# Longer unbroken runs of the dense products, and other TensorE times in the planner, in a hybrid attention and delta-rule layer

## The chip, the cores and the metric

One core of a Trainium2 chip runs the kernel. The metric is the device time of one execution in microseconds. The engines of the core are TensorE (PE, matmuls; PEld is its weight load), VectorE (DVE), ScalarE (ACT), GpSimd (POOL) and SyncE (SP, which issues DMAs). Each engine works through its own list of instructions in order, and waits at an instruction whose operands are not there.

## What is computed

A decoder layer on 512 tokens and 16 meta tokens, width 1024. Two branches of eight heads each run on the same normalised input: differential softmax attention, and a gated delta rule in chunks. Their gated outputs are merged and projected.

```python
proj = hn @ w_in
aq, ak, av, az, dq, dk, dv, dz, db, da, ga, gd = split(proj)
# attention branch, per head: two softmaxes, their difference times v
pd = p[:, :, 0] - lam * p[:, :, 1]
y_a = (rms_norm(pd @ v) * (1 - lam_init) * silu(az)) @ w_branch_attn
# delta branch: causal convolution of width 4, silu, normalised q and k, then in chunks
m = where(strict, (kb @ k.T) * decay, 0)
t_inv = triangular_solve(m + eye, eye)
u = t_inv @ (v * beta);  w = t_inv @ (kb * exp(gc))
# over the chunks, one after the other
v_new = u - w @ state
o = q_dec @ state + a_intra @ v_new
state = state * chunk_decay + k_dec.T @ v_new
y_d = (rms_norm(o) * silu(dz)) @ w_branch_delta
merged = sigmoid(ga) * y_a + sigmoid(gd) * y_d
out = rms_norm(h + merged @ w_out)
```

## The kernel before

**Products.** Each dense product takes one block of 128 columns of the weights (name and number in `ORDER`, such as dz(2): the delta branch's gate of head 2). Input and weights are split in a high and a low part (`hnH`, `hnL`; `wh` made by ScalarE, `wl` by VectorE, line 383), and three passes of 8 matmuls each make one accumulator: 24 matmuls for a segment of tokens. Gates and queries take one segment of 512 columns; keys and values two, of 272 and 256. `dense()` (line 1580) makes the products one after the other: for each pair of heads g dk, dv, dq of both heads, then ak, aq, az, av of head 2g, then dz(2g) and dz(2g+1), then ak, aq, az, av of head 2g+1. After the four pairs come gd and yd (the delta branch's output product), ga and ya, and the output projection. The generator yields the engine ahead of every three matmuls; between two yields another task may put its own instructions in.

**The delta rule of a pair** (`delta_pair`, line 853). `MT` holds the products of keys with keys times the decay `E`, evacuated by VectorE; it goes to DRAM (`scrm`) and comes back in another layout (`msub`). VectorE then inverts triangular blocks of 32 x 32 by substitution: 31 steps of two operations (`tmps`, `ts`), each needing the one before. The result goes by DRAM (`scrt`) to `td`. The first matmuls on it are `td,MT`; blocks of 64 and 128 (`TT`), the chunks (`vin`, `u`, state `S`) and the output follow: ScalarE copies to `MT`, squares, VectorE reduces and scales, TensorE transposes (`ident,MT`), VectorE makes `od`. `qT<-qT,eg` multiplies the queries by the decay `eg`, which a DMA broadcasts from DRAM (`gcd`) once `eg`'s one buffer is free.

**The two ends.** `branch` (line 1508) splits `od` in `brH` (ScalarE) and `brL` (VectorE) for yd. The buffers for it lie in a pool that opens when all four pairs are done (`pools`, line 1691), so all eight splits follow the last `od`.

**What sets the order.** `Plan` (line 75) is a list scheduler, run while the kernel is built: at each point the task goes on that can start soonest by an estimate of the instructions' times (`Engine.time`, line 220), and of several that of the lowest rank. Delta tasks have rank 0, attention 2, the dense products 4, so they fill what the others leave. The order that results is fixed in each engine's list. The estimates have no part in the run itself. In the profile, helper line 216 stands for every instruction issued through `Engine`.

Of the kernel before, what the change touches and what calls it, by code (L numbers as in the profile page):

```python
# [20 lines left out]
KB = D // P  # L21
# [15 lines left out]
def dense_order():  # L37
    """Products with weight blocks of 128 columns, in the order in which they are made."""
    order = []
    for g in range(H // 2):  # L40
        for n in ("dk", "dv", "dq"):
            order += [(n, 2 * g), (n, 2 * g + 1)]
        order += [(n, 2 * g) for n in ("ak", "aq", "az", "av")]
        order += [("dz", 2 * g), ("dz", 2 * g + 1)]
        order += [(n, 2 * g + 1) for n in ("ak", "aq", "az", "av")]
    for g, y in (("gd", "yd"), ("ga", "ya")):
        order += [(g, c) for c in range(AHEAD)]
        for c in range(KB):
            order += [(y, c)] + [(g, c + AHEAD)] * (c + AHEAD < KB)
    return order  # L50
# [4 lines left out]

# how many of the accumulators serve a purpose at most, and how many there are
BANKS = dict(pd=2, pat=2, pdl=2)
# [4 lines left out]

# tiles of each kind, and accumulators, that are in use at a time
SLOTS = dict(raw=3, w=2, wo=4, psc=1, xp=2, y=2, kT=2, qT=2, ktd=2, vr=2, E=2, eg=1, AT=2, MT=2, sc=2, km=1,
             ts=1, msub=1, TT=1, aq=2, ak=1, vT=1, vs=1, e=4, pT=2, pm=2, ao=1, br=8, th=4)


# until when the tensor engine's clock runs at half its rate
COLD = 10500
# [8 lines left out]
class Plan:  # L78
    """Puts the instructions of many tasks in one order, which all engines keep.

    A task is a generator. It yields the engine that its next instructions are for and then emits them; or an event's
    name, to wait for that; or (name,), to wait for one of some slots. The task that can start soonest goes on, by an
    estimate of the instructions' times in ns; of several, the one of the lowest rank.
    """

# [11 lines left out]
    def here(self):  # L97
        """When and where that is done which the running task has emitted."""
        if self.arrival:
            return self.arrival, SP  # L100
        return (self.end, self.engine) if self.engine else (self.task.time, self.task.src)
# [44 lines left out]
    def settle(self):  # L146
        """Lets every task go on that waits for what is there."""
        moved = True
        while moved:
            moved = False  # L150
            for task in sorted(self.tasks, key=lambda t: t.rank):
                if task.want == ():
                    self.wait(task, (0.0, SP))
                elif isinstance(task.want, tuple):
                    kind = task.want[0]
                    free = self.slots["bank" if kind in self.kinds else kind]
                    if not free or self.kinds.get(kind) == 0:
                        continue
                    if kind in self.kinds:
                        self.kinds[kind] -= 1  # L160
                    free.sort()
                    *since, task.slot = free.pop(0)
                    self.wait(task, tuple(since))
                elif task.want in self.events:
                    self.wait(task, self.events[task.want])
                else:
                    continue
                moved = True
# [22 lines left out]
class Banks(list):  # L191
    """The accumulators of a product, in the order in which they are done."""

# [7 lines left out]
class Engine:  # L201
    """An engine whose instructions' times are estimated as they are emitted."""

# [16 lines left out]
    def time(self, op, args, kw):  # L220
# [4 lines left out]
        n = int(np.prod(out.shape[1:]))  # L225
        if self.name == PE:
# [3 lines left out]
            if dt == F32:  # L230
                small = ins[0].shape[0] <= 64
                return 2 * max(2 * n / 2.4, 27 if small else 107)
            if dt == F32R:
                return n / 2.4 + 2.7 if n >= 256 else max(2 * n / 2.4, 107)
            return n / 2.4 + 57
# [15 lines left out]
def hybrid_block(ctx: ExitStack, tc: tile.TileContext, x, meta, wblk, wbd, wout, pcol, prow, out):  # L251
# [30 lines left out]
    def bank(kind):  # L282
        """An accumulator, two banks for scores, else one: that which the running task has taken."""
        return mk(ps, [P, 2, 512], F32, kind, SLOTS[kind]) if kind == "psc" else banks_[plan.task.slot]
# [16 lines left out]

    # ---------------------------------------------------------------- constants
    nwb = mk(sp, [P, D], F32, "nwb")
# [75 lines left out]

    # ---------------------------------------------------------------- loads  # L380
    weights = {}

    def split(n, raw):
        """Weights as high and low parts."""
        if n < len(ORDER) or n - len(ORDER) in (4, 5):
# [52 lines left out]

    # ---------------------------------------------------------------- hn, transposed, as high and low parts
    hn = [hnp.tile([P, KB, L], F32R, tag=t, name=t) for t in ("hnH", "hnL")]  # L440

    def normalise(n):
        """The meta tokens lie as (part of the channels, token) on the partitions, the others by token."""
        yield f"x{n}"
# [53 lines left out]

    # ---------------------------------------------------------------- gates of the delta rule, all heads
    FULL = [(0, 272), (272, 256)]  # L500
# [11 lines left out]
    def gates():  # L512
# [137 lines left out]
        spawn(rows())  # L650
        # the meta tokens of two heads lie on 32 partitions
        msel = gt("msel", (32, 8, 2))
# [47 lines left out]

    # ---------------------------------------------------------------- what follows a projection
    od = [rp.tile([P, SEQ], F32, tag=f"od{h}", name=f"od{h}") for h in range(H)]
# [10 lines left out]
    def conv_silu(banks, chan, t_lo, dst_tag, tags=("pd", "pd")):  # L713
        """2 silu(conv(projection)) from t_lo on, in a tile of dst_tag or in that returned second, else scratch"""
        n = L - t_lo
# [45 lines left out]
    def after_gate(h, banks, dst, event):  # L761
        """dst = 2 silu(projection)"""
        pd = banks[0][0]
# [85 lines left out]

    # ---------------------------------------------------------------- the delta rule, two heads at a time  # L850
    kt_, s_, sd_, vs_, qe_ = 0, 1, 2, 3, 4

    def delta_pair(gi):
# [14 lines left out]
        def decay(i):  # L868
            """exp(gc_j - gc_i), keys on partitions"""
            h = hs[i]  # L870
# [16 lines left out]
        def keys(i):  # L887
# [23 lines left out]
            def decayed():  # L911
                """The keys' part in the state at the end of their chunk"""
                for c in range(NC):
# [184 lines left out]

        # inverses of the unit triangular 32 x 32 blocks, a block and half its columns on a partition
        yield ("ts",)  # L1100
# [39 lines left out]
        tdt, tdmt = mk(dp, [P, 8, 32], F32, "tdt", 1), mk(dp, [32, 32], F32, "tdmt", 1)  # L1140
        # blocks of 32 to 64 to 128, transposed; x is head and chunk
        TT = slot(dp, [P, 8, P], F32, "TT")
# [213 lines left out]

    # ---------------------------------------------------------------- differential attention, one head
    def attention(h):
# [11 lines left out]
        def combine(i, st, es):  # L1370
# [7 lines left out]
            give("e")  # L1378
            # the meta tokens' part, of which a high part, a high part and a low part lie beside one another
            yield ("pm",)  # L1380
# [118 lines left out]

    # ---------------------------------------------------------------- the dense products  # L1500
    def again(tag, dt=F32):
# [6 lines left out]
    def branch(h, of, name):  # L1508
        """A branch's result as high and low parts."""
        yield f"{'od' if name == 'yd' else 'oa'}{h}"  # L1510
# [42 lines left out]
    def first_products():  # L1553
        """The first two products, in parts that follow the tokens' arrival."""
        yield ("psc",)
# [24 lines left out]
    def dense():  # L1580
        yield from first_products()
        for n, (name, i) in list(enumerate(ORDER))[2:]:
# [6 lines left out]
            for t0, nn in SEGS.get(name, BODY):  # L1589
                yield ("pd",)  # L1590
                pd = None
                for k in range(KB):
                    yield PE
                    pd = bank("pd")[:, :nn] if k == 0 else pd
# [16 lines left out]
            if name in ("yd", "ya"):  # L1611
                tick(name, KB)
                if i == KB - 1:
                    for _ in range(H):
                        give("br")
        # the output projection, the residual and the last norm
        yield "gp"
# [24 lines left out]
    def finish(hf, tb, c0, c1, pd, tag, ssq, fnw, xr):  # L1642
        """The residual's sum and its square's; with the last columns of some tokens, their norm"""
        t = xr[hf, tb][:, c0:c1]
# [15 lines left out]
        spawn(weigh(), 2)  # L1660
        # of the sums so far, but the last: mean + eps
        if col == 0:
# [28 lines left out]
    def pools():  # L1691
        """The pools that take the place of those of the two branches."""
        yield "delta"
# [41 lines left out]
def layout(inputs):  # L1735
    """The inputs as the program reads them: moved, and nothing else."""
    f = {k: np.asarray(v) for k, v in inputs.items()}
# [41 lines left out]
```

## Time and profile before

| | |
|---|---|
| three runs | 787.58, 789.86, 791.32 us (median 789.86) |
| the profiled execution's span | 787.3 us |
| TensorE's first product matmul, last matmul's end | 7.8 us, 781.1 us |
| VectorE, ScalarE, GpSimd busy | 541.8, 383.3, 76.1 us |
| substitutions (first `tmps` to last `ts`), us from the start | 90.0 to 128.4, 227.4 to 262.4, 355.4 to 392.5, 489.3 to 525.5 |
| first `td,MT` of each pair | 136.9, 272.0, 401.1, 533.2 us |

The profiled execution has a span and no time of its own beside it; the runs' times are of other executions. A window row gives a stretch in us from the start and, per engine, how long it was busy in it. A wait row has the total, the number and the longest. A timeline row has start, duration, engine, line, operation, output<-inputs, shapes and count, and in brackets the idle time ahead of it with what ended it. Matmuls overlap, so that a matmul's duration (0.39 us) is longer than the distance to the next one.

### The profile page before, as it was taken

Reading aid. Unit: us, or ns where it says so; the run is one execution under the profiler, and the core shown is the slowest. Engines: PE = TensorE matmul, PEld = TensorE weight load, DVE = VectorE, ACT = ScalarE, POOL = GpSimd, SP = SyncE. Lnnn points to the kernel's source line nnn. Section 1 sums busy time; section 2 is a strip of 40 time slices with the busy share of each in tenths; the row PEclk is TensorE's granted clock in tenths of the full one; section 3 lists DMA queues with packets and bytes.
Section 4 is the critical chain, followed back from the end, with each engine's and each line's share of the span. In section 5 each row is a group of like instructions: output and inputs, shape, how many; then the busy total and the mean of one; then the engine's idle time right before and its main releaser. Section 6 shows DMA issues by size and latency. Waiting matters only on the chain.

```text
span 787.3 us, 13576 instructions
## 1 busy us (share of the span) xinstructions
PE 761.1 (97%) x5191; PEld 682.8 (87%) x5191; DVE 541.8 (69%) x1279; ACT 383.3 (49%) x944; POOL 76.1 (10%) x114
## 2 busy tenths in 40 slices
PE   5999999999999999999999999899999999999996
PEld 4999878999988899987999998788888888888886
DVE  6788697788779778859968875995772334335643
ACT  5374535576545557553557744355562224223322
POOL 3120002021100301100030201000000000000001
PEclk9999999999999999999999999999999999999999
DMA  7132624202352401272240125233116232233402
GB/s 274 40 110 84 152 81 110 68 28 82 95 141 81 122 28 55 67 153 83 81 110 28 56 90 119 81 94 83 51 62 235 80 108 88 100 100 112 136 1 107
DMA packets 46744, 74.36 MB, mean 94 GB/s; under 512 B 20528, under 2 KB 29136, under 8 KB 46680
## 3 DMA queue, kind: packets, MB, share of 16 engines
q1 hardware_dynamic: 45400, 69.18, 29.3%
q0 software_dynamic: 1280, 4.33, 2.5%
q8 instruction: 40, 0.66, 0.3%
q14 instruction: 24, 0.20, 0.1%
HBM read 65.98 MB, written 3.19 MB: 88 GB/s over the span
## 4 chain that ended last, share of the span: by engine, by line
PE 57%; DMA 5%; DVE 4%; issue 1%; ACT 1%; SPq 1%; POOL 1%; POOLq 0%; DVEq 0%; ACTq 0%
PE bank L216 55%; DMA msub<-scrm 2%; PE psc L216 2%; DVE wl L216 1%; DMA scrt<-ts 1%; DMA td<-scrt 1%; SPq L216 1%; DVE tmps L216 1%; DVE ts L216 1%; DMA eg<-gcd 1%; DMA scrm<-MT 1%; DVE aq L216 0%; POOL ts L216 0%; DVE MT L216 0%; ACT wh L216 0%
## 5 line engine op out<-in xcount | busy, mean ns | idle before, releaser
L216 PE MATMUL bank<-hnH,wh 128*128 128x512 f32 (+3 forms) x944 | 317.6, 339 | 1.4 <-ACT hnH L216 0.8
L216 PE MATMUL bank<-hnH,wl 128*128 128x512 f32 (+3 forms) x944 | 302.9, 323 | 3.7 <-DVE wl L216 3.7
L216 PE MATMUL bank<-hnL,wh 128*128 128x512 f32 (+3 forms) x944 | 302.4, 323 | 0.0
L216 PEld LDWEIGHTS bank<-hnH,wl 128*128 128x128 f32 x944 | 177.7, 189 | 19.6 <-DVE wl L216 5.5
L216 PEld LDWEIGHTS bank<-hnH,wh 128*128 128x128 f32 x944 | 177.8, 189 | 15.0 <-ACT hnH L216 1.0
L216 PEld LDWEIGHTS bank<-hnL,wh 128*128 128x128 f32 x944 | 178.0, 190 | 11.1
L216 ACT CAST wh<-raw 128x1024 fp32r<-128x1024 f32 x98 | 102.8, 1049 | 127.0 <-PE bank L216 116.2
L216 DVE TENSOR_TENSOR wl<-raw,wh 128x1024 fp32r<-128x1024 f32 x98 | 120.0, 1225 | 61.4 <-ACT wh L216 60.8
L216 DVE SCALAR_TENSOR_TENSOR y<-xp,pc,y 128x528 f32<-128x528 f32 (+1 forms) x72 | 54.3, 755 | 0.8 <-ACT y L216 0.2
L216 PE MATMUL bank<-brH,wh 128*128 128x512 f32 x128 | 50.1, 392 | 0.0
L216 PE MATMUL bank<-brL,wh 128*128 128x512 f32 x128 | 49.8, 389 | 0.0
L216 PE MATMUL bank<-brH,wl 128*128 128x512 f32 x128 | 49.8, 389 | 0.0
L216 ACT ACTIVATE e<-psc,ast 128x144 f32<-128x144 f32 (+3 forms) x64 | 34.4, 541 | 30.3 <-DVE ast L216 26.2
L216 DVE TENSOR_TENSOR tmps<-msub,ts 97x240 f32<-97x240 f32 (+27 forms) x124 | 39.5, 319 | 5.9 <-DMA msub<-scrm 4.1
L216 DVE TENSOR_TENSOR ts<-ts,tmps 97x240 f32<-97x240 f32 (+27 forms) x124 | 39.6, 320 | 1.8
L216 PE MATMUL psc<-ak,aq 128*128 128x264 f32 (+3 forms) x160 | 29.1, 304 | 4.3 <-ACT e L216 4.3
L216 POOL DMA_DIRECT2D ak<-ak x16 | 8.8, 551 | 219.5 <-DVE ak L216 161.2
L216 PEld LDWEIGHTS psc<-ak,aq 128*128 128x128 f32 x160 | 23.6, 189 | 7.2 <-ACT e L216 6.0
L216 DVE SCALAR_TENSOR_TENSOR od<-th,bank 128x512 f32<-128x512 f32 x16 | 10.9, 684 | 26.6 <-PE bank L216 26.6
L216 DVE TENSOR_REDUCE ast<-psc 128x1 f32<-128x528 f32 (+3 forms) x40 | 28.5, 713 | 0.2
L216 PEld LDWEIGHTS bank<-brH,wh 128*128 128x128 f32 x128 | 24.0, 188 | 5.1
L216 PEld LDWEIGHTS bank<-brH,wl 128*128 128x128 f32 x128 | 24.0, 188 | 5.1
(299 smaller groups left out, 1214.6 us busy)
## 6 DMA issues: line engine op xcount, KB each, us to landing
raw<-in_wblk_dram SPq DMA_DIRECT2D x96, 512.0 KB, 3.5
ak<-ak POOLq DMA_DIRECT2D x16, 264.0 KB, 4.3
raw<-in_wout_dram SPq DMA_DIRECT2D x8, 512.0 KB, 3.7
xt<-in_x_dram SPq DMA_DIRECT2D x4, 512.0 KB, 3.6
E<-gcd SPq DMA_DIRECT2D x8, 256.0 KB, 5.7
eg<-gcd SPq DMA_DIRECT2D x8, 256.0 KB
xr<-in_x_dram SPq DMA_DIRECT2D x8, 256.0 KB, 6.5
out_dram<-xr SPq DMA_DIRECT2D x8, 256.0 KB, 2.1
```

The source lines that it names most:

```text
L216: return real(*args, **kw)
```

## The change

All comments and docstrings are taken out, which moves lines (216 becomes 219) and nothing else. A constant `RUN = 4` is new. `dense()` yields to the planner less often: ahead of each segment of under 512 tokens once (24 matmuls in one run), and in a product of 512 tokens ahead of every fourth k (two runs of 12). The planner's estimates for TensorE's matmuls are other numbers: 512 columns 231.8 ns (216 before), 272 columns 125 (116), 256 columns 117.9 (109.4), and three nanoseconds more on each of the two passes of a float32 matmul. Slots, ranks, the other engines' estimates and what is computed stay.

```diff
+RUN = 4
...
             if dt == F32:
                 small = ins[0].shape[0] <= 64
-                return 2 * max(2 * n / 2.4, 27 if small else 107)
+                return 2 * max(2 * n / 2.4 + 3, 27 if small else 110)
             if dt == F32R:
-                return n / 2.4 + 2.7 if n >= 256 else max(2 * n / 2.4, 107)
+                return 0.445 * n + 4 if n >= 240 else 111
...
                 for k in range(KB):
-                    yield PE
+                    if k % (KB if nn < 512 else RUN) == 0:
+                        yield PE
                     pd = bank("pd")[:, :nn] if k == 0 else pd
```

Since the planner makes the order, the change shows in the engines' lists. Three places of them follow. A row is an instruction: the line, the operation, output<-inputs with the number of the tile, and the shape.

**TensorE at the first `td,MT`, pair 0.** Before: it stands behind all of av(1) (`wh_1534` is av(1)'s weight block, here the end of its second segment).

```order
L216 MATMUL bank_6_83<-hnH,wl_1536 128x256
L216 MATMUL bank_5_82<-ident,pm_87_618 96x128
L216 MATMUL bank_6_83<-hnH,wh_1534 128x256
L216 MATMUL bank_6_83<-hnL,wh_1534 128x256
L216 MATMUL bank_6_83<-hnH,wl_1536 128x256
L216 MATMUL bank_1_78<-td_1604,MT_953 32x32 x4
L216 MATMUL bank_1_78<-td_1604,MT_997 32x32 x4
```

After: the block ahead of it is az(1)'s (512 columns), followed by scores of head 1's attention.

```order
L219 MATMUL bank_6_83<-hnH,wh_1458 128x512
L219 MATMUL bank_6_83<-hnL,wh_1458 128x512
L219 MATMUL bank_6_83<-hnH,wl_1460 128x512
L219 MATMUL psc_1607<-ak_1020,aq_1075 128x264 x4
L219 MATMUL bank_4_81<-td_1555,MT_946 32x32 x4
L219 MATMUL bank_4_81<-td_1555,MT_996 32x32 x4
```

The 48 matmuls of av(1) have moved from ahead of `td,MT` to behind it. In the other pairs `td,MT` stood inside the next pair's dk(4) (pair 1) or inside av's second segment (pairs 2 and 3); now it stands ahead of av(2g+1) in all of them.

**VectorE at the last evacuations of `MT`, pair 0.** `MT_997` before and `MT_996` after are that of head 1; `qT_918` and `qT_901` are the queries of head 0; `E_1014` and `E_1003` the decay of the next pair. Before:

```order
L216 SCALAR_TENSOR_TENSOR MT_997<-bank_3_80,sc_635,E_651 128x128
L216 TENSOR_TENSOR ak_1029<-vT_939,ak_1029 64x528
L216 SCALAR_TENSOR_TENSOR MT_997<-bank_3_80,sc_635,E_651 128x128
L216 SCALAR_TENSOR_TENSOR MT_997<-bank_5_82,sc_635,E_651 128x128
L216 TENSOR_TENSOR AT_998<-bank_3_80,E_651 128x256
L216 SCALAR_TENSOR_TENSOR MT_997<-bank_5_82,sc_635,E_651 128x128
L216 TENSOR_TENSOR ak_1029<-vT_939,ak_1029 64x528
L216 TENSOR_TENSOR qT_918<-qT_918,eg_1018 128x512
L216 TENSOR_SCALAR E_1014<-E_1014,gc 128x128
```

After, from the second evacuation on:

```order
L219 SCALAR_TENSOR_TENSOR MT_996<-bank_3_80,sc_638,E_654 128x128
L219 TENSOR_TENSOR ak_1020<-vT_934,ak_1020 64x528
L219 TENSOR_TENSOR AT_997<-bank_3_80,E_654 128x256
L219 TENSOR_SCALAR sc_638<-sc_638 128x4
L219 TENSOR_TENSOR qT_901<-qT_901,eg_1004 128x512
L219 TENSOR_SCALAR E_1003<-E_1003,gc 128x128
L219 TENSOR_TENSOR ak_1020<-vT_934,ak_1020 64x528
L219 TENSOR_SCALAR E_1003<-E_1003,gc 128x128
L219 SCALAR_TENSOR_TENSOR MT_996<-bank_5_82,sc_638,E_654 128x128
L219 TENSOR_SCALAR E_1003<-E_1003,gc 128x128
L219 SCALAR_TENSOR_TENSOR MT_996<-bank_5_82,sc_638,E_654 128x128
```

The product with `eg` and three rows of the next decay have moved ahead of the last two evacuations.

**TensorE at the end of the delta rule.** Before, from the last transposes `ident,MT` to product yd(0) (`brH`); `wh_6739` is gd(2), `wh_6869` gd(3), of which the rows of one step are shown.

```order
L216 MATMUL bank_2_79<-ident,MT_5857 128x128 x4
L216 MATMUL bank_4_81<-ident,pm_86_617 96x128
L216 MATMUL bank_1_78<-hnH,wh_6739 128x512
L216 MATMUL bank_1_78<-hnL,wh_6739 128x512
L216 MATMUL bank_1_78<-hnH,wl_6741 128x512
L216 MATMUL bank_4_81<-vm_619,pmT_6924 128x128
L216 MATMUL bank_4_81<-vs_6629,pT_6923 128x128 x3
L216 MATMUL bank_3_80<-hnH,wh_6869 128x512
L216 MATMUL bank_3_80<-hnL,wh_6869 128x512
L216 MATMUL bank_3_80<-hnH,wl_6871 128x512
```

After, from the state's product of the last chunk to yd(0); `wh_6842` is the weight block of yd(0):

```order
L219 MATMUL bank_4_81<-S_6880,qT_5790 128x128
L219 MATMUL bank_4_81<-u_6958,AT_5826 128x128
L219 MATMUL bank_1_78<-ident,e_6815 128x128 x3
L219 MATMUL bank_6_83<-ident,pm_86_627 96x128
L219 MATMUL bank_6_83<-vm_628,pmT_6935 128x128
L219 MATMUL bank_6_83<-vs_6653,pT_6934 128x128 x3
L219 MATMUL bank_3_80<-ident,MT_5825 128x128 x4
L219 MATMUL bank_2_79<-ident,e_6893 128x128 x4
L219 MATMUL bank_4_81<-ident,pm_85_626 96x128
L219 MATMUL bank_4_81<-vm_628,pmT_7000 128x128
L219 MATMUL bank_4_81<-vs_6653,pT_6999 128x128 x4
L219 MATMUL bank_5_82<-brH_7014,wh_6842 128x512
```

The 24 matmuls of gd(3) have moved from behind the last `ident,MT` to ahead of the last chunk's `vin,TT`.

## The prediction

> **What bounds the kernel now.** I read the engine shares on the page first, then its chain, then TensorE's waits, then windows. Times of steps are us from the start of the profiled execution.
>
> ```profile
> span 787.3 us, 13576 instructions
> PE 761.1 (97%) x5191; PEld 682.8 (87%) x5191; DVE 541.8 (69%) x1279; ACT 383.3 (49%) x944; POOL 76.1 (10%) x114
> PE 57%; DMA 5%; DVE 4%; issue 1%; ACT 1%; SPq 1%; POOL 1%; POOLq 0%; DVEq 0%; ACTq 0%
> ```
>
> TensorE is busy 97% of the span. The matmuls are the same after the change, so its work stays; what can move is the time in which it waits. The chain leaves TensorE for some 10% of the span, through DMA and VectorE. TensorE's largest waits behind its start, and two ways to count them by stage (20 us windows; below them windows from the first matmul of product dz(2g), g the head pair, to the first td,MT):
>
> ```profile
> PE psc L216 <- ACT e L216: 4.3, 3, 1.9
> PE bank L216 <- DVE wl L216: 3.7, 4, 1.5
> PE bank L216 <- DMA td<-scrt: 1.4, 3, 0.7
> ```
>
> ```profile
> 100.00:120.00 20.00, 18.10 (x101) 15.67 (x100) 18.60 (x54) 7.59 (x23) 0.00 (x0) 0.91 0.27 84
> 500.00:520.00 20.00, 18.67 (x113) 16.32 (x112) 19.69 (x61) 7.97 (x25) 0.00 (x0) 1.00 0.29 97
> 600.00:620.00 20.00, 20.00 (x89) 16.34 (x88) 5.59 (x5) 4.23 (x6) 0.00 (x0) 1.00 0.36 113
> 92.10:136.90 44.80, 42.55 (x248) 36.74 (x246) 39.01 (x107) 20.36 (x51) 5.11 (x8) 0.96 0.34 93
> 225.60:272.00 46.40, 44.42 (x277) 38.91 (x275) 40.55 (x113) 23.91 (x57) 5.41 (x8) 1.00 0.36 99
> 357.20:401.10 43.90, 42.08 (x243) 36.20 (x241) 39.94 (x110) 21.62 (x52) 4.65 (x7) 0.96 0.32 93
> 490.80:533.20 42.40, 38.83 (x229) 33.26 (x228) 38.30 (x107) 19.04 (x47) 1.02 (x2) 1.00 0.33 92
> ```
>
> The columns are the window, its length, then busy us of PE, PEld, DVE, ACT, POOL, and the granted clock. In 500:520 VectorE is busy 19.69 of 20 us: this is the substitution (62 rows tmps and ts, each using the one before), with the weight splits wl, softmax and scores between its rows. There, four times in the kernel, VectorE sets the pace. In 600:620 it is busy 5.59 and TensorE all 20.00.
>
> **Longer runs.** The deleted comments emit nothing. A step of three matmuls becomes one of 12 or 24. What a switch between products costs TensorE is in the spacing of starts:
>
> ```profile
> 93.66 0.39 PE L216 MATMUL bank<-hnH,wh 128*128 128x512 f32 x1
> 93.90 0.39 PE L216 MATMUL bank<-hnL,wh 128*128 128x512 f32 x1
> 130.14 0.29 PE L216 MATMUL bank<-hnL,wh 128*128 128x272 f32 x1
> 132.91 0.29 PE L216 MATMUL bank<-hnH,wl 128*128 128x272 f32 x1
> ```
>
> 512 columns take 0.231 us here (0.24 in this pair, 20.00/89 = 0.225 in 600:620), 272 columns (132.91 − 130.14)/22 = 0.126, and 256 columns 0.118, all inside runs already. Over the listing a matmul behind a switch is late by at most 0.01 us, and 200 switches vanish at most: 0 to −2, taken −0.5. The planner's new figures, 0.232 and 0.125, fit these rows; the old, 0.216 and 0.116, were 7% short.
>
> The Trainium skill, page "TensorE: Matmul & The Clock Gate", section "Back-to-back issue gap", gives columns/2.4 + 2.5 ns, 0.216 us at 512: the planner's old number. The rows above (0.225 to 0.24) do not agree, and by that rule alone the new costs would be the worse ones; the sum here doesn't use it.
>
> **The substitution's result comes sooner in TensorE's queue.** td,MT takes the substitution's result by DRAM. By the listings, between dz(2g)'s first matmul and td,MT there stood, in pair 0, 96 of 512 columns (dz, dz, aq, az), ak's 24 + 24, av's 24 + 24 and 48 small ones: 96 x 0.231 + 2 x 24 x (0.126 + 0.118) + 48 x 0.13 = 40.1. In pairs 1 to 3: 43.5 (with 18 of dk besides), 39.3 and 37.8 (9 of av's second part). After, av stands behind td,MT in every pair, with 31 to 35 small ones before it: **32.4, 32.4, 32.4, 31.9**. The windows took 44.8, 46.4, 43.9, 42.4, so 4.7, 2.9, 4.6, 4.6, in all **16.8 us**, are waits, small gaps and a lower clock (0.91 in 100:120: half speed for 3.4 us, 1.7 lost; the same once in pair 2). Work ahead of the substitution is the same in both.
>
> So TensorE will be at td,MT 5.4 to 11 us sooner. Is its input there? Before:
>
> ```profile
> 81.04 0.69 DVE L216 TENSOR_TENSOR qT<-qT,eg 128x512 f32<-128x512 f32 x1 [3.55 <-ACT eg L216]
> 76.42 0.34 DVE L216 SCALAR_TENSOR_TENSOR MT<-bank,sc,E 128x128 f32<-128x128 f32 x1
> 82.26 0.29 DVE L216 TENSOR_SCALAR E<-E,gc 128x128 f32<-128x128 f32 x1 [0.53 <-DMA E<-gcd]
> 90.00 0.19 DVE L216 TENSOR_TENSOR tmps<-msub,ts 97x31 f32<-97x31 f32 x1 [0.32 <-DMA msub<-scrm]
> 128.20 0.17 DVE L216 TENSOR_TENSOR ts<-ts,tmps 97x16 f32<-97x16 f32 x1
> 227.36 0.18 DVE L216 TENSOR_TENSOR tmps<-msub,ts 97x31 f32<-97x31 f32 x1
> 262.27 0.17 DVE L216 TENSOR_TENSOR ts<-ts,tmps 97x16 f32<-97x16 f32 x1
> 355.44 0.19 DVE L216 TENSOR_TENSOR tmps<-msub,ts 97x31 f32<-97x31 f32 x1 [2.56 <-DMA msub<-scrm]
> 392.34 0.18 DVE L216 TENSOR_TENSOR ts<-ts,tmps 97x16 f32<-97x16 f32 x1
> 489.26 0.19 DVE L216 TENSOR_TENSOR tmps<-msub,ts 97x31 f32<-97x31 f32 x1 [1.25 <-DMA msub<-scrm]
> 525.32 0.17 DVE L216 TENSOR_TENSOR ts<-ts,tmps 97x16 f32<-97x16 f32 x1
> 136.91 0.87 PE L216 MATMUL bank<-td,MT 32*32 32x32 f32 x25 [0.36 <-DMA td<-scrt]
> 533.16 0.81 PE L216 MATMUL bank<-td,MT 32*32 32x32 f32 x23 [0.69 <-DMA td<-scrt]
> ```
>
> The input came just when TensorE did: the waits there are 0.36 and 0.69. Its path has three lengths.
>
> Start: last MT evacuation, scrm to DRAM, msub back, then tmps. Pair 0: 76.76 to 90.00, 13.2 us; the others 13.1, 13.8, 12.4. After, in pair 0, qT stands ahead of the second head's last two MT, and qT waits for the transfer eg (3.55 here), with E's transfer behind it. qT's end at 81.73, two E, ak (0.7), MT at 0.3 each put the last MT at 83.3 instead of 76.8, the substitution at 83.3 + 13.2 = 96.5; if eg came sooner by 5.0, which is its mean wait, 91.5. Nothing decides between them: I take the middle, 94.0. In pair 2 qT moves ahead too, with two E: 0.69 + 2 x 0.28 = +1.2, 356.6. In pairs 1 and 3 it stood there before; fewer rows ahead of MT give −1.8 (225.6) and −0.2 (489.1).
>
> Length: 38.4, 35.1, 37.1, 36.2. The listing has 106 other rows in the four substitutions instead of 142; 36 rows at some 0.45 us are 16 us. By pair 31.0, 32.0, 32.1, 32.5.
>
> End to td,MT: through scrt, 136.91 − 128.37 = 8.5; 9.6, 8.6 and 7.7 in the others.
>
> Input against TensorE's arrival:
> pair 0: 94.0 + 31.0 + 8.5 = 133.5, arrival 92.1 + 32.4 = 124.5, wait 9.0.
> pair 1: 225.6 + 32.0 + 9.6 = 267.2 against 258.0, wait 9.2.
> pair 2: 356.6 + 32.1 + 8.6 = 397.3 against 389.6, wait 7.7.
> pair 3: 489.1 + 32.5 + 7.7 = 529.3 against 522.7, wait 6.6.
> In all 32.5. The old 16.8 lie ahead of td,MT and are swallowed; so is a later weight split wl (in pair 1 that of dz(2) now stands behind the first rows tmps), as long as TensorE waits less than 9 us for it. So the difference is **+15.7**. TensorE's in-order queue holds av(2g+1), dk and dv of the next pair behind td,MT: none can fill the wait. The bounds: each substitution 3 us sooner, +3.7; 2 us later, +23.7.
>
> The skill's same page, section "Part 1: The HAM clock gate", has the clock halved after an idle window of about 3.4 us; 0.91 in 100:120 agrees. After waits of 7 to 9 us it would add up to 1.7 us each, 7 in all, inside the range.
>
> **The end of the delta rule.** Before, gd3's 24 matmuls (5.5 us) stood behind the last transposes ident,MT and covered the split of od into brH and brL, which yd0 reads; after, gd3 is done ahead of the last chunk's vin,TT.
>
> ```profile
> 565.06 0.38 PE L216 MATMUL bank<-vin,TT 128*128 128x128 f32 x2
> 568.33 0.27 ACT L216 COPY MT<-bank 128x128 f32<-128x128 f32 x1 [0.15 <-PE bank L216]
> 571.44 0.69 DVE L216 TENSOR_TENSOR MT<-MT,co 128x512 f32<-128x512 f32 x1 [0.32 <-POOL co L216]
> 572.93 0.60 PE L216 MATMUL bank<-ident,MT 128*128 128x128 f32 x4
> 575.10 3.22 ACT L216 CAST brH<-od 128x512 fp32r<-128x512 f32 x6
> ```
>
> From MT's copy to brH 6.8 us, one brH 0.5, and from vin,TT to the copy 2 (3.3 here, with dense matmuls between) make 9.3 us, against 5.2 us of matmuls that are left there: **+4**, between +1 (copies overlap better) and +6.
>
> **The steps behind td,MT** (level blocks, squares, chunks) stand behind 12 or 24 matmuls instead of 3, so their operands are more often there: small gaps of 0 to 4 us go, taken −2.
>
> Sum: 787.3 + 15.7 + 4 − 2 − 0.5 = 804.5. The three runs' median, 789.9, is 2.6 above the profiled span: **807**.
>
> **Rivals.** (A) The forecast, own range 799 to 818: 0.62; above it 0.04. (B) The substitutions start 3 us sooner each, as msub's transfers have less beside them, and the tail costs 1: 787.3 + 3.7 + 1 − 2.5 + 2.6 = 792; 0.15 between 792 and 799. For it: DMA waits in the rows above (2.56, 1.25) that a sooner MT shortens; against: eg's wait now stands in front. (C) Faster: the truer plan takes the wl, psc and td waits out, because the input of td,MT is there when TensorE comes. That needs each substitution 8 us sooner at its end than in A, and decides from about 4 us sooner, where the waits sum to the old 16.8. Then 787.3 − 16.8 + 4 − 2.5 + 2.6 = 775: 0.12, range 772 to 786. For it: VectorE's length is a sum of rows, and with TensorE never ahead of it the splits may fall out of the loop; against: msub takes 13 us of DMA that the planner does not see. (D) The change does nothing that counts: td's wait only takes the place of the wl and psc waits, the tail is covered, 787 to 793: 0.07.
>
> **How the numbers follow.** A measurement of this kernel tells about 0.5% from no change, 786 to 794. Faster is C, 0.12; the same is D and the low edge of B, 0.10; slower 0.78. The range goes from 788, which leaves out C, to 818, which leaves out 0.04.
>
> **What would show it.** Right: PE waits for DMA td<-scrt of 6 to 9 us in each of four places in place of 0.4 to 0.7; the wl and psc waits ahead of them smaller; in pair 0 the first tmps at 91.5 to 96.5; PE waiting for brH or od at yd0 some 4 us; 512-column spacing unchanged. Wrong: td's waits under 4 us each, which makes it B, C or D, or a first tmps before 88.

## The result and the profile after

The changed kernel takes 826.2 us (median of four runs, 823.5 to 828.8) against 790.5 for the kernel before: a ratio of 1.047, 95% interval 1.045 to 1.050. It is slower by some 36 us; I forecast 17, and a range up to 818. Executions of one kernel can differ by their granted clock, and the ratios leave out those over 1.5% above the kernel's fastest: there are three, all of before_dma below (792 to 797 us at a clock of 0.98, its others 779 to 782 at 1.00). The profiled execution of the changed kernel is the longest of its four. Its page, with the lines for span, engines and chain:

```profile
span 827.0 us, 13602 instructions
PE 776.7 (94%) x5191; PEld 693.5 (84%) x5191; DVE 547.0 (66%) x1279; ACT 381.2 (46%) x944; POOL 82.7 (10%) x114
PE 54%; DVE 18%; DMA 8%; ACT 4%; issue 3%; SPq 2%; POOL 2%; POOLq 0%; DVEq 0%; ACTq 0%
```

The number of instructions on each engine is as before and VectorE's work has grown by only 5 us, but the chain now spends 18% of the span on VectorE (4% before). TensorE's largest waits (total, times, longest) behind its start, and that for td:

```profile
PE bank L219 <- DVE wl L219: 7.5, 4, 2.9
PE bank L219 <- ACT pmT L219: 7.5, 2, 4.8
PE psc L219 <- ACT e L219: 6.4, 4, 2.8
PE bank L219 <- ACT wh L219: 3.9, 3, 2.0
PE bank L219 <- ACT TT L219: 3.2, 3, 1.1
PE bank L219 <- DMA td<-scrt: 0.2, 1, 0.2
```

The wait for td, which I expected to hold 6 to 9 us in each pair, is 0.2 us in all. To see where the time went I worked out from both traces what each stretch takes beyond the sum of its matmuls' usual spacings (0.231 us for 512 columns, the kernel's own median for other kinds). This *excess* holds waits, small gaps and stretches in which the granted clock was half (*half clock*):

| stretch (us of excess) | before | changed | difference | forecast |
|---|---|---|---|---|
| 24 us to dz(0) | 1.7 | 1.1 | −0.6 | 0 |
| dz(2g) to td,MT, four pairs | 16.5 | 29.6 | +13.1 | +15.7 |
| td,MT to dz(2g+2), three pairs | 3.7 | 16.7 | +13.0 | −2 |
| last td,MT to yd(0) | 1.7 | 15.0 | +13.3 | +4 |
| behind yd(0) | −1.2 | −0.4 | +0.8 | 0 |

The differences add to 39.6, and the spans differ by 39.7. So three stretches lose 13 us each, of which I had one about right in size.

**Ahead of td,MT.** The timeline of the changed kernel in pair 0, rows of ScalarE, VectorE and TensorE:

```profile
91.97 0.63 ACT L219 ACTIVATE eg<-eg 128x512 f32<-128x512 f32 x1 [4.99 <-DMA eg<-gcd]
92.50 1.03 ACT L219 CAST wh<-raw 128x1024 fp32r<-128x1024 f32 x1
...
92.63 0.69 DVE L219 TENSOR_TENSOR qT<-qT,eg 128x512 f32<-128x512 f32 x1 [4.92 <-ACT eg L219]
94.34 0.19 DVE L219 TENSOR_TENSOR tmps<-msub,ts 97x31 f32<-97x31 f32 x1 [0.80 <-DMA msub<-scrm]
95.97 1.22 DVE L219 TENSOR_TENSOR wl<-raw,wh 128x1024 fp32r<-128x1024 f32 x1
...
93.59 0.51 PE L219 MATMUL bank<-hnH,wh 128*128 128x512 f32 x1 [2.02 <-ACT wh L219]
97.25 0.80 PE L219 MATMUL bank<-hnH,wl 128*128 128x512 f32 x1 [2.92 <-DVE wl L219]
133.65 0.97 PE L219 MATMUL bank<-td,MT 32*32 32x32 f32 x29 [0.19 <-DMA td<-scrt]
```

The input of td,MT came at 133.65; my estimate was 133.5. But TensorE had waited already: the weight split wh of dz(0) stands behind the exponential of eg on ScalarE, which waits 4.99 us for its transfer, and wl stands behind the first rows of the substitution on VectorE, which wait for msub. TensorE stands 2.0 and 2.9 us at dz(0)'s first matmuls, and comes to td,MT just when its input does. Over the four pairs its waits from dz(2g) to td,MT went from 9.6 to 19.9 us, the half clock there from 6.8 to 13.6 us, which costs up to half of that.

**Behind td,MT.** The rows of TensorE in the changed kernel from a matmul of the delta chain to the next, a run of 24 between them, of which the first and last two are shown, and then VectorE's `vin`, which the last one needs:

```profile
180.12 0.39 PE L219 MATMUL bank<-u,AT 128*128 128x128 f32 x2
180.27 0.37 PE L219 MATMUL bank<-hnH,wh 128*128 128x272 f32 x1
...
183.12 0.29 PE L219 MATMUL bank<-hnL,wh 128*128 128x272 f32 x1
183.24 0.29 PE L219 MATMUL bank<-hnH,wl 128*128 128x272 f32 x1
183.37 0.60 PE L219 MATMUL bank<-ident,kT 128*128 128x128 f32 x4
183.80 0.39 PE L219 MATMUL bank<-vin,TT 128*128 128x128 f32 x2
...
180.10 0.35 DVE L219 SCALAR_TENSOR_TENSOR vin<-bank,negegc,vr 128x128 f32<-128x128 f32 x1
```

`vin` is done at 180.45, and the matmul that takes it starts at 183.80. Over all 32 chunks it starts 2.0 us after `vin` in the mean; before, 0.47. TensorE is busy in that time, so no wait row shows it. What it does is lengthen the chain (what that costs is another question, answered further down): from the first td,MT to the end of the pair's last od it took 40.0, 36.0, 39.4 and 41.7 us before, and takes 70.4, 73.8, 70.7 and 60.8 now. The rows of pair 0, before and changed (td,MT starts at 136.91 and 133.65):

```profile
175.46 1.47 DVE L216 SCALAR_TENSOR_TENSOR od<-bank,wD,od 128x512 f32<-128x512 f32 x2
```

```profile
203.34 0.75 DVE L219 SCALAR_TENSOR_TENSOR od<-bank,wD,od 128x512 f32<-128x512 f32 x1 [0.23 <-PE bank L219]
```

**The end.** The timeline of TensorE and ScalarE in the changed kernel ahead of yd(0), and then the window (us, busy PE, PEld, DVE, ACT, POOL, granted clock, DMA):

```profile
610.00 0.47 PE L219 MATMUL bank<-vm,pmT 96*128 96x128 f32 x1 [2.75 <-ACT pmT L219]
613.48 0.42 PE L219 MATMUL bank<-ident,pm 128*96 128x128 f32 x1
618.67 0.47 PE L219 MATMUL bank<-vm,pmT 96*128 96x128 f32 x1 [4.77 <-ACT pmT L219]
...
614.20 4.25 ACT L219 CAST brH<-od 128x512 fp32r<-128x512 f32 x8
618.36 0.26 ACT L219 CAST pmT<-bank 96x128 fp32r<-96x128 f32 x1
```

```profile
600.00:620.00 20.00, 12.48 (x74) 11.12 (x73) 15.40 (x33) 11.97 (x32) 2.01 (x2) 0.74 0.20 66
```

The last od is late, no dense matmul is left to cover it, and the two lists cross: TensorE has a matmul of the attention ahead of yd(0) whose input pmT stands on ScalarE behind all eight splits brH: that is the wait of 4.77 us. The pmT of the wait of 2.75 us comes ahead of them. TensorE is busy 12.48 of 20 us, at a granted clock of 0.74.

### The profile page after: what moved, and what is told of

The parts are those of the page before. It is cut to its first block, busy times and chain, and to the rows that moved or that the text cites. A ratio compares the mean times of both kernels' runs of the same rounds, so it can differ in the third digit from the quotient of the medians.

```text
span 827.0 us, 13602 instructions
## 1 busy us (share of the span) xinstructions
PE 776.7 (94%) x5191; PEld 693.5 (84%) x5191; DVE 547.0 (66%) x1279; ACT 381.2 (46%) x944; POOL 82.7 (10%) x114
## 4 chain that ended last, share of the span: by engine, by line
PE 54%; DVE 18%; DMA 8%; ACT 4%; issue 3%; SPq 2%; POOL 2%; POOLq 0%; DVEq 0%; ACTq 0%
PE bank L219 53%; DMA msub<-scrm 4%; DVE ts L219 4%; DVE tmps L219 4%; DVE wl L219 3%; DVE ast L219 2%; DMA eg<-gcd 2%; SPq L219 2%; PE psc L219 1%; POOL ts L219 1%; DMA E<-gcd 1%; DMA scrt<-ts 1%; ACT TT L219 1%; ACT wh L219 1%; DVE od L219 1%
## 5 line engine op out<-in xcount | busy, mean ns | idle before, releaser
L219 PE MATMUL bank<-hnH,wh 128*128 128x512 f32 (+3 forms) x944 | 313.3, 334 | 4.7 <-ACT wh L219 3.9
L219 PEld LDWEIGHTS bank<-hnH,wl 128*128 128x128 f32 x944 | 179.9, 191 | 23.5 <-DVE wl L219 9.3
L219 PEld LDWEIGHTS bank<-hnH,wh 128*128 128x128 f32 x944 | 180.1, 192 | 19.5 <-ACT wh L219 4.5
L219 PEld LDWEIGHTS bank<-hnL,wh 128*128 128x128 f32 x944 | 180.0, 192 | 12.5
L219 DVE TENSOR_TENSOR tmps<-msub,ts 97x240 f32<-97x240 f32 (+27 forms) x124 | 39.7, 320 | 6.8 <-DMA msub<-scrm 4.6
L219 ACT COPY xp<-bank 128x258 f32<-128x258 f32 (+2 forms) x46 | 17.4, 378 | 29.1 <-PE bank L219 27.1
L219 PEld LDWEIGHTS bank<-brL,wh 128*128 128x128 f32 x128 | 24.3, 190 | 5.1
```

Source lines behind the costliest of these rows:

```text
L219: return real(*args, **kw)
```

## The experiments

All are against the kernel before, run on the same chip. The ratio is of medians with its 95% interval; excess and chain are worked out as above; the clock is the mean granted clock of the profiled execution. (1 − clock) x span is my estimate of the most that half clock can have cost there: 5 us before, 20 in the changed kernel, 31 in runs_only and r512. A kernel's own medians grow with its half clock, so that the excess is too small where the clock is low: the rows of nudge and costs_only account for 6 us less than their spans differ from that of before (13 and 27 us). In short:

| kernel | us | ratio (interval) | clock | dz to td | td to dz | to yd(0) | chain, pairs 0 to 2; 3 |
|---|---|---|---|---|---|---|---|
| before | 790 | | 0.994 | 16.5 | 3.7 | 1.7 | 36 to 40; 42 |
| changed | 826.2 | 1.047 (1.045 to 1.050) | 0.976 | 29.6 | 16.7 | 15.0 | 70 to 74; 61 |
| runs_only | 833.3 | 1.053 (1.049 to 1.057) | 0.963 | 18.7 | 28.2 | 12.1 | 61 to 62; 55 |
| costs_only | 808.5 | 1.025 (1.019 to 1.030) | 0.973 | 30.1 | 5.4 | 7.2 | 42 to 46; 47 |
| nudge | 797.9 | 1.010 (1.006 to 1.013) | 0.982 | 14.9 | 13.1 | 0.5 | 40 to 45; 40 |
| gd_fine | 815.9 | 1.032 (1.028 to 1.035) | 0.983 | 29.9 | 16.4 | 3.8 | 70 to 74; 44 |
| run2 | 811.5 | 1.028 (1.027 to 1.030) | 0.987 | 23.4 | 12.9 | 1.4 | 49; 48 |
| seg_whole | 810.0 | 1.026 (1.025 to 1.028) | 0.988 | 5.3 | 30.9 | 1.1 | 58 to 59; 41 |
| r512 | 828.7 | 1.052 (1.048 to 1.057) | 0.963 | 24.1 | 13.4 | 11.9 | 38 to 44; 60 |
| costs_dma | 783.1 | 0.994 (0.990 to 0.997) | 0.993 | 3.4 | 11.6 | 2.2 | 38 to 43; 42 |
| before_dma | 787.3 | 0.988 (0.985 to 0.991) | 0.998 | 8.9 | 4.3 | 1.8 | 39; 37 |
| after_dma | 812.6 | 1.030 (1.027 to 1.032) | 0.978 | 3.6 | 24.8 | 13.0 | 60 to 61; 56 |
| runs_beside | 782.2 | 0.992 (0.990 to 0.995) | 0.996 | 5.6 | 9.1 | 2.0 | 39 to 40; 40 |

### The two halves of the change

runs_only keeps the run rule and the old TensorE times; costs_only the new times and a yield ahead of every three matmuls.

```diff
 # runs_only, against the changed kernel
-                return 0.445 * n + 4 if n >= 240 else 111
+                return n / 2.4 + 2.7 if n >= 256 else max(2 * n / 2.4, 107)
 # (and the float32 line as before)
 # costs_only, against the changed kernel
-                    if k % (KB if nn < 512 else RUN) == 0:
+                    if True:
```

> The run rule alone, with the planner's old TensorE times. Theory S (two separate causes): the runs take away the cover behind td,MT (+10 us in the changed kernel between td,MT and the next dz) and at the end of the delta rule (+13); the substitution's stretch stays as before, since td,MT stands 39 to 40 us of work behind dz(2g) again. So 790 + 20 to 25, about 812. Theory C (all by the new times): 788 to 793. Theory R (all by the runs): 824 to 828.

> The planner's new TensorE times alone, dense products in steps of three matmuls as before. Theory S: td,MT stands 32 to 34 us of work behind dz(2g), so the four stretches from dz(2g) to td,MT lose 15 us more than before in waits and half clock (wh, wl, psc, td), and nothing is lost behind td,MT or at the end: about 805. Theory C: 824 to 828. Theory R: 788 to 793.

Measured: 833.3 and 808.5. Each half costs, so C and R fall. costs_only is as S had it: ahead of td,MT its excess is 30.1, like the changed kernel's. That little is lost behind it is less sure: its profiled execution was 7 us longer than its other runs, with half clock for 10.2 us behind td,MT of pair 0 and for 13.7 us behind that of pair 3, so the 7.2 at its end may be high. runs_only loses where S said, behind td,MT and at the end, but 44 us in place of 20 to 25: 28.2 behind td,MT, 12.1 at the end, and 4.6 more ahead of dz(0); S had left out the clock, which can stand for some 26 us of it. The two halves don't add (44 + 20 against 36 together), since each makes another order.

### How much any reordering is worth

```diff
-                return n / 2.4 + 2.7 if n >= 256 else max(2 * n / 2.4, 107)
+                return n / 2.4 + 3.0 if n >= 256 else max(2 * n / 2.4, 107)
```

> The kernel before with one planner figure moved by 0.3 ns (512 columns 216.3 instead of 216.0), which reorders parts of it. It shows how much any reordering is worth. Theories S, C and R: 786 to 796. If chance in the order is what decides (theory N): anything from 775 to 826, above 800 would speak for it.

Measured: 797.9 (ten runs, 791 to 803). Just above what S allowed, and under N's 800. Most of this 1% goes with the clock: the three runs with a clock of 0.992 or more took 791 to 794 us, the five at 0.980 to 0.984 took 799 to 803. The kernel before had 0.987 to 0.999 in its thirteen runs beside these. In the profiled execution of nudge half clock stands right behind td,MT of pairs 1 and 2, for 13.7 us each. Its windows from td,MT to the first vin,TT, pair 0 and pair 1:

```profile
135.30:148.30 13.00, 12.97 (x181) 11.92 (x182) 8.60 (x22) 7.41 (x19) 1.74 (x3) 1.00 0.26 70
271.00:289.30 18.30, 17.09 (x168) 15.69 (x169) 9.87 (x29) 5.88 (x18) 2.81 (x4) 0.66 0.08 26
```

The change is worth 4.7%, so chance in the order, with the clock that comes with it, is a part of such a result, and not the most of it.

### The end of the delta rule

```diff
-                    if k % (KB if nn < 512 else RUN) == 0:
+                    if name == "gd" or k % (KB if nn < 512 else RUN) == 0:
```

> The changed kernel with the four products gd (and the next four) in steps of three matmuls again; all other products keep the long runs. Theory S: some 60 dense matmuls stand between the last chunks and yd(0) again, the waits for pmT of 2.8 and 4.8 us and the half clock there go, the rest stays: 826 - 10 to 13, about 814. If the end of the delta rule costs only its 4 us of my forecast: 822. Theory C: no change, 826.

Measured: 815.9, 10.3 less than the changed kernel, as S had it. The excess ahead of yd(0) falls from 15.0 to 3.8 and the chain of pair 3 from 61 to 44 us, while the other stretches and chains of its row stay. Both waits for pmT there are gone. The edit doesn't shorten a matmul; it lets the chain's matmuls in between. The chain then ends sooner, and some dense matmuls are left to stand beside its last steps.

### The length of a run, and which products have them

With old TensorE times: runs of 6 in all products (run2), whole segments of 24 alone (seg_whole), runs of 12 in the products of 512 alone (r512). The section on the kernel before says that queries take one segment of 512 columns. That holds for the attention's aq; the delta rule's dq take two of 258 (`SEGS`), so that they are in threes in r512, and in runs of 24 in seg_whole.

```diff
 # run2
+                    if k % 2 == 0:
 # seg_whole
+                    if nn == 512 or k == 0:
 # r512
+                    if nn < 512 or k % RUN == 0:
```

> The run rule alone with runs of 6 matmuls everywhere (1.4 us of 512 columns, 0.75 us of 272), old TensorE times. Theory Q (queueing: each matmul of the delta chain waits for the rest of the run ahead of it, on average half of one): the chain from td,MT to the pair's last od, 36 to 42 us before and 55 to 62 with long runs, comes to 43 to 50, and the time to 797 to 808. Rival O (only the length of a whole segment or a chance order matters): chain 36 to 42 and 787 to 795.

> Old TensorE times; only the segments of 256 and 272 tokens in one run of 24 (2.8 to 3.0 us), products of 512 tokens in threes. Theory Q: the chain behind td,MT, beside av, dk and dv, is stretched nearly as in the run with both (50 to 60 us in pairs 0 to 2), the end of the delta rule beside gd is not (38 to 46 us in pair 3, no waits there): 808 to 820. Rival E (the end of the delta rule is what the runs cost): 787 to 796.

> Old TensorE times; only products of 512 tokens in two runs of 12 (2.8 us), the segments in threes. Theory Q: the chain is stretched where it stands beside dq and gd (45 to 55 us in pairs 0 to 2, 50 to 56 in pair 3), waits of 8 to 12 us at the end of the delta rule: 805 to 820. Rival E: 803 to 808, all of it ahead of yd(0).

Measured: 811.5, 810.0, 828.7. The chains are where Q had them in run2 (48 to 49) and seg_whole (58 to 59 in pairs 0 to 2, 41 in pair 3): the products whose runs are long stretch the chain that stands beside them, and by the length of the run. r512 stretches pair 3 to 60, beside gd, more than I gave, and pairs 0 to 2 hardly (38 to 44 in place of 45 to 55): I had counted dq among the products of 512, and in r512's trace no matmul of 512 columns stands beside the chain of these pairs. The times of run2 and r512 lie above what I expected (797 to 808, 805 to 820). Both lose 7 us ahead of td,MT, which Q says nothing of, and r512's clock of 0.963 can stand for some 26 us of the 40 that it loses. Rival O falls by run2's chain and time, E by seg_whole, which loses 30.9 behind td,MT and nothing at the end. The largest waits of TensorE in seg_whole:

```profile
PE bank L219 <- DVE ao L219: 10.3, 3, 4.5
PE bank L219 <- ACT sq L219: 7.5, 1, 7.5
PE bank L219 <- ACT ktd L219: 7.1, 4, 3.3
```

(sq is the start of the kernel, in every kernel alike.) The waits of 10.3 are for a result of the attention. They stand at 234, 374 and 503 us, over 20 us behind the pair's last od, so how the longer chain would bring them about isn't shown. Of the 7.1 for ktd the longest, 3.3, stands at 64 us, ahead of the first td,MT, where there is no chain yet; the others, 1.3 each, stand in the chain's last steps.

### The transfers that the planner takes for done too soon

costs_dma is costs_only with three arrival times set nearer to the trace; before_dma and after_dma are the kernel before and the changed one with the same lines.

```diff
             S.dma_start(out=e, in_=gc_row(h))
+            plan.arrival += 3500
             S.dma_start(out=eg, in_=gc_row(h))
+            plan.arrival += 3500
                 S.dma_start(out=msub[o:o + 33], in_=scr)
+                plan.arrival += 5000
```

> The planner's new TensorE times with steps of three, and its arrival times of the transfers E, eg (+3.5 us) and msub (+5 us) set nearer to the trace. Theory D (the new TensorE times cost because the planner takes these transfers for done too soon, and so puts the splits wh and wl of dz(2g) behind the waits for them): the waits for wh, wl of 1.3 to 3.7 us at dz(2g) fall below 1.5 us each, and the time from 808 to 790 to 798. Rival T (the truer TensorE times cost by td,MT standing too soon, whatever the transfers): 804 to 812.

> The kernel before with the arrival times of E, eg and msub set nearer to the trace and the old TensorE times: the fourth corner of new TensorE times against true arrivals. Theory D (the two errors of the old planner cancelled, so that mending one alone costs): slower than before, 792 to 805, with td,MT 44 to 45 us of work behind dz(2g). Rival G (true arrivals gain by themselves, whatever the TensorE times): 780 to 786.

> The changed kernel with those arrival times. Theory Q: the waits ahead of td,MT go as they did with steps of three, the delta chain stays at 55 to 75 us and the end of the delta rule uncovered: 805 to 818. Rival H (the long runs cost only by what the arrivals misplace): 780 to 792.

costs_dma: 783.1, better than I gave, and again 785.0 in more runs. The timeline of its ScalarE and VectorE in pair 0, with the split of dz(0) first, and then TensorE's waits, of which this is the largest behind the start:

```profile
85.90 1.04 ACT L219 CAST wh<-raw 128x1024 fp32r<-128x1024 f32 x1
87.24 0.63 ACT L219 ACTIVATE eg<-eg 128x512 f32<-128x512 f32 x1 [0.30 <-DMA eg<-gcd]
...
86.97 1.23 DVE L219 TENSOR_TENSOR wl<-raw,wh 128x1024 fp32r<-128x1024 f32 x1 [1.64 <-ACT wh L219]
88.11 0.68 DVE L219 TENSOR_TENSOR qT<-qT,eg 128x512 f32<-128x512 f32 x1
88.85 0.19 DVE L219 TENSOR_TENSOR tmps<-msub,ts 97x31 f32<-97x31 f32 x1
```

```profile
PE bank L219 <- DMA td<-scrt: 1.8, 1, 1.8
```

wh and wl stand ahead of the wait for eg, which is 0.30 us now. No wait for wh or wl is among TensorE's largest any more, and the excess ahead of td,MT goes from 30.1 to 3.4. The same new TensorE times that cost 20 us are harmless once the transfers are true: theory D's first half is shown, and T falls. Its second half, that the old planner's two errors cancelled and mending the arrivals alone would cost, is not: before_dma's ratio of 0.988 is 780 us, as G had it. But its ratio rests on three runs, so its gain is the least certain of all here. after_dma came out as Q said, at 812.6: the waits ahead of td,MT go (3.6), the chain stays at 56 to 61 us, and the end is uncovered again (13.0). So the long runs cost 28 to 30 us by themselves, with those arrivals true; the clock, 0.978 against 0.993, can stand for 12 of them. H falls.

### Long runs where no chain waits

```diff
 # against costs_dma
-                    if True:
+                    if k % (KB if nn < 512 else RUN) == 0 or not (name == "dz" or (name in ("ak", "aq", "az") and i % 2)):
```

> New TensorE times, true arrivals, and long runs only in the products that stand beside the substitution (dz, and ak, aq, az of the odd head), where no matmul of the delta chain waits; all others in threes. Theory Q: the chain keeps its 37 to 45 us, and neither cost nor gain: 780 to 788, the same as without long runs. If long runs cost wherever they stand: 795 or more; if they gain by fewer switches: under 780.

> The fastest kernel so far once more with more rounds: new TensorE times, true arrivals, steps of three. 780 to 786 if its 0.6% is real, 787 to 791 if not.

Measured: 782.2 and 785.0, ratios 0.992 (0.990 to 0.995) and 0.995 (0.993 to 0.997). The chain keeps 39 to 40 us. Beside the substitution, where TensorE has no matmul of the chain to let through, long runs do no harm; a gain from them can't be told from none. Both kernels are faster than both of the case, by 0.5 to 0.8% against the one before.

## Why the prediction was wrong

**The step that failed** is "The steps behind td,MT … stand behind 12 or 24 matmuls instead of 3, so their operands are more often there: small gaps of 0 to 4 us go, taken −2". It has the effect the wrong way round: the stretch gained 13.0 us of excess in place of losing 2. A step that is made to wait until its operands are sure to be there is a step that is late, and these steps depend on each other, so the chain grew from 40 to 70 us. In the listings I had counted the places of td,MT and of gd3, but not how many dense matmuls stand ahead of each link of the chain. TensorE's busy share hides it as well, as the 3.35 us between `vin` and its matmul show.

Where the time goes is not the same as where the chain grows. The excess of pairs 0 to 2 once more, now by the medians of the kernel before for every kernel, in three parts; in brackets what half clock can have cost of it:

| us | td,MT to first vin,TT | to the last od | to dz(2g+2) |
|---|---|---|---|
| before | 2.4 | 1.1 | 1.0 |
| changed | 10.3 (3.4) | 5.1 | 3.1 |
| after_dma | 19.3 (10.2) | 8.1 | 1.1 |
| seg_whole | 2.9 | 13.8 | 16.0 (6.8) |
| costs_dma | 9.9 (5.1) | 1.3 | 1.4 |
| nudge | 15.6 (12.1) | 2.4 (1.5) | 1.0 |
| r512 | 19.3 (15.3) | 0.6 | 1.7 |

In the chunks (the middle part) excess over 3 us comes only with runs of 24 beside the chain, 4.0 of the changed kernel's 14.0. Most of the rest lies ahead of the chunks, in the small matmuls behind td,MT: there the changed kernel has a wait of 1.1 us for TT in each of the three pairs and half clock in one, and kernels without a run beside the chain (the last three rows) lose about as much or more, over half of which half clock can stand for. So it is not shown that the long runs made all of these 13 us, nor that they did it by the length of the chain.

**The end of the delta rule** was right in its mechanism (nothing left to cover the od of the last pair), and mis-sized: 13.3 in place of 4. I counted the path from the last vin,TT and took the matmuls there for the cover; the chain as a whole came later, TensorE's list crossed ScalarE's at pmT (4.8 of 7.5 us of waits), and the clock fell to 0.74; half clock can have cost 7.5 us between td,MT of pair 3 and yd(0). gd_fine shows that the long runs of gd are the cause.

**td,MT sooner in the queue** was +15.7 and is +13.1. The input's time was right in pair 0 to 0.2 us, in part by luck: I took the middle of 91.5 and 96.5, where 91.5 rests on a mean wait for eg of 5.0 us that is 2.8 in the trace (22.6 us in eight), and the substitution took 32.3 us instead of 31.0, the way from it to td,MT 7.0 instead of 8.5. Its form was wrong, and that the sum came near is luck too: I wrote of the waits ahead of td,MT that they were swallowed by its wait; it was the other way, and the waits for wh, wl and psc grew, came first and left td,MT 0.2 us. I named wl behind the substitution's first rows, but only for pair 1, and didn't see wh behind eg on ScalarE. My sign for "wrong" (td's waits under 4 us make it B, C or D) therefore pointed to 799 us or less when all the waiting had only moved ahead. costs_only puts this term on the new TensorE times, and costs_dma on their meeting transfers that are counted too short.

**Longer runs**, 0 to −2 taken as −0.5, can stand, as far as tried: runs_beside, with long runs in a part of the products, against costs_dma_again is −2.8 us in the medians, with intervals that overlap.

The clock took part too, a term that the sum put at nothing: the mean granted clock was 0.976, before 0.994, which is up to 15 of the 39.7 us between the two profiled executions (3.4 from dz(2g) to td,MT, 3.4 from there to dz(2g+2), 7.5 ahead of yd(0), 1.0 behind it). The prediction kept up to 7 us for it, after waits of 7 to 9 us. No such waits came, and none are needed: its own example, 0.91 in 100:120, is half clock for 3.4 us behind a wait of 1.90. The Trainium skill, page "TensorE: Matmul & The Clock Gate", section "A second HAM failure mode: psum-queue depth-cycling", says that frequent short idle times between groups of matmuls can be enough to halve the clock. This window of the changed kernel agrees, at 0.50, behind small matmuls and waits of at most 1.1 us:

```profile
284.00:288.00 4.00, 4.00 (x20) 4.00 (x20) 0.43 (x1) 0.26 (x1) 0.00 (x0) 0.50 0.27 56
```

What stays open: why the two halves together (826) cost less than the runs alone (833); how far the small waits behind td,MT come from the long runs and how far from any other order; and what brings half clock about there.

## What to carry to other kernels

Work that fills gaps has to be cut finer than the steps that it stands beside: on an engine that works through its list in order, a filler of 2.9 us makes link after link of a dependent chain wait for its rest, and the chain grows by many fillers (30 us here), not by one. A busy engine shows no wait for this, so measure the chain from its first to its last step. The kernel pays for it where nothing is left to cover the chain's end (the last pair: 11 us of excess, by gd_fine), and much less where dense work follows (4 us in the chunks of three pairs). Before a per cent is put down to an order, compare the granted clocks of the runs. And a planner's estimates hold as a set: before one is made truer, look at which others (here the transfers) it will be compared with.

## What the runs showed that I had not expected

A planner's figure moved by 0.3 ns changed the time by 1.0% (0.6 to 1.3%), and by 0.3 to 0.6% in the three runs with a clock of 0.992 or more. A waiting engine can hold up a part that has nothing to do with the wait: ScalarE's 4.99 us for eg cost TensorE 2.0 us for a weight split queued behind it. And in nudge TensorE was granted half clock for 13.7 us at a time behind waits of at most 1.2 us.
